# Rotated queries and keys: transposed on VectorE in blocks of 32 by 32, with the blocks moved by DMA through DRAM

## The chip, the cores and the metric

The kernel runs on one core of one Trainium2 chip. The metric is device time in microseconds (us) of one execution; lower is better. All inputs and outputs are float32.

## The reference, cut to what matters

Two blocks of two layers each, at 256 tokens and width 2048. The change touches the first block alone, whose layers hold a differential attention (8 heads, two queries and two keys of 128 each), a stick-breaking attention (16 heads of 128), two branch projections with gates and an output projection. What is computed around the change:

```python
def rms_norm(x, gain):
    xf = x.astype(jnp.float32)
    y = xf * lax.rsqrt(jnp.mean(xf * xf, axis=-1, keepdims=True) + RMS_EPS)
    return (y * gain.astype(jnp.float32)).astype(x.dtype)

def rope(x):
    ...
    x1, x2 = xf[..., : d // 2], xf[..., d // 2:]
    return jnp.concatenate([x1 * cos - x2 * sin, x2 * cos + x1 * sin], axis=-1).astype(x.dtype)

# hybrid_layer
    q = rope(rms_norm(da_q.reshape(b, s, 2 * DA_HEADS, DA_QK_DIM), qk_q_gain))
    k = rope(rms_norm(da_k.reshape(b, s, 2 * DA_HEADS, DA_QK_DIM), qk_k_gain))
    q = (q * (DA_QK_DIM ** -0.5)).reshape(b, s, DA_HEADS, 2, DA_QK_DIM)
    k = k.reshape(b, s, DA_HEADS, 2, DA_QK_DIM)
    ...
    oa = differential_attention(q[:, :, :, 0, :], q[:, :, :, 1, :],
                                k[:, :, :, 0, :], k[:, :, :, 1, :], va, lam)
# differential_attention, a block of 128 queries
        def probs(qb, kt):
            s = jnp.einsum('bhqd,bhkd->bhqk', qb, kt, preferred_element_type=jnp.float32)
            return jax.nn.softmax(jnp.where(causal, s, MASK_VALUE), axis=-1)
        a = probs(qb1, k1t) - lam * probs(qb2, k2t)
        return jnp.einsum('bhqk,bhkd->bhqd', a.astype(vt.dtype), vt)
```

## The kernel before

**Weights.** Every projection streams its weights from DRAM in halves of 512 KB (128 partitions x 1024 columns). `weights` (L71 to L89) loads a half into `raw` (3 buffers) with a DMA that SyncE's queue (SP) issues (L85), ScalarE (ACT) rounds it into `hi` (4 buffers, L86), and VectorE (DVE) writes the remainder into `lo` (4 buffers, L87). A product is made of three matmuls: activations' high part with `hi`, high part with `lo`, low part with `hi`.

**The projections.** `xstat` (L92 to L108) holds the activations still and streams weights: a half gives 12 matmuls of 512 columns (L104 to L106) into an accumulator of two PSUM banks (`acc`, 2 buffers). After each half it calls `tick`. `wstat` (L112) does the same with weights held still; it makes the projections that are wanted with columns on the partitions.

**Ticks.** Attention is written as Python generators that are started with `spawn` and advanced one step by every `tick` (L63), so that their instructions are written between the matmuls of projections. A step is a stretch between two `yield`s. The framework orders all instructions ahead of time from the written order, taken as priority, and from its own model of when each is ready: an engine's list can take an instruction earlier than it is written. Weights have a priority of 400 instructions ahead (L74). Each engine then runs its list in order and waits on semaphores; SP's list holds nearly all DMAs.

**A layer of the first block.** For each of four pairs of heads `layer` (L537) projects q, k, v and z with `xstat` (four times eight halves). After q it starts `da_pair` (L435), which waits for what it needs: it rotates q, then k when `"k"` is there, makes the scores and the probabilities (`da_probs`, L334), evicts v (`evict_v`, L384) and z (`da_gz`), and makes the output (`da_out`). Its result `ua` is read first after four more projections of gates (32 halves).

**A rotation.** `da_rot` (L295) takes the accumulator of one projection (two blocks of 128 tokens, 4 heads of 128 columns). ACT squares it (L304), DVE makes the two products and their sum (L306 to L313) and the sum of squares (L312), GpSimd (POOL) the inverse root (L316 to L318), and for keys DVE scales the rows (L324). Then, for each block of tokens, PE transposes four 128x128 tiles with the identity into a PSUM bank (L329), and ACT copies the bank into `out`, which is `qkT` with columns on the partitions (L330). The scores (L342, L343) read `qkT`.

In a layer there are 8 rotations; the second block has none.

Of the kernel before, what the change touches and what calls it, by code (L numbers as in the profile page):

```python
# [11 lines left out]
F32 = mybir.dt.float32  # L12
# [6 lines left out]
P = 128  # L19
# [15 lines left out]
def bc(ap, shape, axis):  # L35
    return ap.unsqueeze(axis).to_broadcast(shape)
# [133 lines left out]
class Block1(Net):  # L170
# [124 lines left out]
    def da_rot(self, acc, tabs, scaled, res):  # L295
        nc = self.nc
        out = self.w4.tile([P, 4, T], F32, tag="w4", name="qkT")
        c = self.sm.tile([P, 2, 4], F32, tag="s8", name="c")
        ssq = self.sm.tile([P, 2, 4], F32, tag="s8", name="ssq")
        rots = []  # L300
        for tb in range(2):
            pv = acc[:, tb, :]
            sq = self.w2.tile([P, 4, P], F32, tag="w2", name="sq")
            nc.scalar.activation(sq, pv.rearrange("p (s d) -> p s d", s=4), AF.Square, scale=self.r[:, tb : tb + 1])  # L304
            t1 = self.w2.tile([P, 4, P], F32, tag="w2", name="t1")
            nc.vector.tensor_tensor(  # L306
                out=t1, in0=pv.rearrange("p (s d) -> p s d", s=4), in1=bc(tabs[0][:, tb, :], [P, 4, P], 1), op=ALU.mult)
            t2 = self.w2.tile([P, 4, 2, 64], F32, tag="w2", name="t2")
            nc.vector.tensor_tensor(
                out=t2, in0=pv.rearrange("p (s h d) -> p s h d", s=4, h=2)[:, :, ::-1, :],  # L310
                in1=bc(tabs[1][:, tb, :].rearrange("p (h d) -> p h d", h=2), [P, 4, 2, 64], 1), op=ALU.mult)
            nc.vector.tensor_reduce(ssq[:, tb, :], sq, AX.X, ALU.add)  # L312
            nc.vector.tensor_tensor(out=t1, in0=t1, in1=t2.rearrange("p s h d -> p s (h d)"), op=ALU.add)  # L313
            rots.append(t1)
            yield
        self.rsqrt(c, ssq, 128.0 * EPS)  # L316
        for tb in range(2):
            nc.gpsimd.tensor_scalar(c[:, tb, :], c[:, tb, :], self.r[:, tb : tb + 1], None, ALU.mult)  # L318
        yield
        yield  # L320
        if scaled:
            for tb in range(2):
                t1 = rots[tb]
                nc.vector.tensor_tensor(out=t1, in0=t1, in1=bc(c[:, tb, :], [P, 4, P], 2), op=ALU.mult)  # L324
            yield
        for tb in range(2):
            pt = self.ps().rearrange("p (s d) -> p s d", s=4)
            for sh in range(4):
                nc.tensor.transpose(pt[:, sh, :], rots[tb][:, sh, :], self.ident)  # L329
            nc.scalar.copy(out[:, :, tb * P : (tb + 1) * P], pt)  # L330
        yield
        res += [out, c]

    def da_probs(self, qT, kT, cq, aTs):  # L334
# [1029 lines left out]
def build(nc, a, out, opts):  # L1364
    with tile.TileContext(nc) as tc, ExitStack() as ctx:
        dram = ctx.enter_context(tc.tile_pool(name="dram", bufs=1, space=bass.MemoryType.DRAM))
        b = Block1(nc, tc, ctx, a)
# [4 lines left out]
            tp=pool(c1, "tp", bufs=1),  # L1372
            w4=pool(c2, "w4", bufs=6, side="right"), w15=pool(c2, "w15", bufs=8, side="right")))
        x1 = dram.tile([P, 16, T], F32, name="x1")
        xt, xs = [b.tt() for _ in range(4)], []
        b.sqs = b.tp.tile([P, 2, T], F32, tag="sqs", name="sqs")

# [189 lines left out]
```

## Time and profile before

| | |
|---|---|
| median of 3 runs | 3277.18 us (3275.35 to 3278.25) |
| the profiled execution | 3272.04 us |
| its span in the trace | 3270.3 us |
| PE / DVE / ACT busy | 99% / 66% / 51% of the span |
| granted TensorE clock | 0.998 of full speed |
| DMA | 573 MB, mean 175 GB/s |

The profile is of one execution. PE is the matmuls on TensorE, PEld its weight loads, DVE VectorE, ACT ScalarE, POOL GpSimd, SP SyncE with its DMA queue. Matmuls overlap and their ends are modelled, so the start of one matmul after the other tells more than their durations. `out<-in` are the program's names, L and a number a line of the kernel. In a timeline a row has the start (us), the time (us), engine, line, operation and, in brackets, how long the engine was idle just before and what ended that.

### The profile page before, as it was taken

How to read it: one execution, taken by the hardware profiler on the slowest of the kernel's cores; microseconds unless marked ns; L12 is line 12 of the kernel's file. 1: busy time of each engine (PE TensorE's matmuls, PEld its weight loads, DVE VectorE, ACT ScalarE, POOL GpSimd, SP SyncE). 2: the span in 40 equal slices, each digit the busy share in tenths (PEclk: the TensorE clock that was granted, in tenths of full speed). 3: DMA queues.
4: the chain of work that ended last, by engine and by line, in shares of the span. 5: the costliest groups of instructions: out<-in, count | busy, mean ns of one | idle time of the engine just before them, and what ended most of it. 6: DMA issues, size and time to landing. Idle time of an engine off the chain costs nothing.

```text
span 3270.3 us, 48437 instructions
## 1 busy us (share of the span) xinstructions
PE 3243.7 (99%) x19158; PEld 2862.2 (88%) x19158; DVE 2173.0 (66%) x2865; ACT 1656.0 (51%) x2321; POOL 253.2 (8%) x227
## 2 busy tenths in 40 slices
PE   9999999999999999999999999999999999999998
PEld 7888888888888888888888888888889999999998
DVE  7666655566665666566655566665678986689865
ACT  5544444444444454444444444444456675466753
POOL 2010100000000001001100000000013000130003
PEclk9999999999999999999999999999999999999999
DMA  6555556555555666555556655555665534555454
GB/s 227 172 170 171 174 181 193 182 174 175 171 176 182 209 204 194 172 172 170 175 178 192 185 175 173 172 176 182 203 190 181 161 121 143 171 166 160 128 166 141
DMA packets 165189, 573.04 MB, mean 175 GB/s; under 512 B 22497, under 2 KB 25441, under 8 KB 164961
## 3 DMA queue, kind: packets, MB, share of 16 engines
q1 hardware_dynamic: 164816, 569.93, 55.3%
q8 instruction: 150, 2.46, 0.3%
q14 instruction: 79, 0.64, 0.1%
q10 hardware_dynamic: 144, 0.02, 0.0%
HBM read 565.68 MB, written 4.19 MB: 174 GB/s over the span
## 4 chain that ended last, share of the span: by engine, by line
PE 92%; DVE 4%; issue 2%; ACT 1%; DMA 1%; POOL 0%; SPq 0%; POOLq 0%; DVEq 0%; ACTq 0%
PE acc L138 29%; PE acc L140 14%; PE acc L106 8%; PE acc L105 8%; PE acc L104 8%; PE acc L131 6%; PE acc L132 6%; PE acc L133 6%; DVE lo L87 1%; PE acc L137 1%; PE ps L379 1%; DMA raw<-wx 0%; PE ps L329 0%; PE ps L343 0%; PE ps L1166 0%
## 5 line engine op out<-in xcount | busy, mean ns | idle before, releaser
L87 DVE TENSOR_TENSOR lo<-raw,hi 128x1024 fp32r<-128x1024 f32 (+1 forms) x1061 | 1318.0, 1243 | 761.1 <-ACT hi L86 758.6
L86 ACT CAST hi<-raw 128x1024 fp32r<-128x1024 f32 (+1 forms) x1061 | 1114.2, 1050 | 1187.3 <-PE acc L138 444.8
L138 PE MATMUL acc<-T,hi 128*128 128x512 f32 x4096 | 1439.9, 397 | 0.0
L140 PE MATMUL acc<-T,lo 128*128 128x256 f32 x3840 | 1077.7, 281 | 0.0
L138 PEld LDWEIGHTS acc<-T,hi 128*128 128x128 f32 x4096 | 762.0, 188 | 171.6
L140 PEld LDWEIGHTS acc<-T,lo 128*128 128x128 f32 x3840 | 725.7, 189 | 5.8
L104 PE MATMUL acc<-hi,T 128*128 128x512 f32 x1280 | 520.7, 407 | 0.3 <-ACT hi L86 0.3
L131 PE MATMUL acc<-T,hi 128*128 128x272 f32 (+2 forms) x1776 | 519.1, 292 | 0.2 <-DVE w L890 0.2
L132 PE MATMUL acc<-T,hi 128*128 128x272 f32 (+2 forms) x1776 | 508.9, 287 | 0.0
L133 PE MATMUL acc<-T,lo 128*128 128x272 f32 (+2 forms) x1776 | 508.9, 287 | 0.0
L105 PE MATMUL acc<-lo,T 128*128 128x512 f32 x1280 | 505.9, 395 | 2.7 <-DVE lo L87 2.7
L106 PE MATMUL acc<-hi,T 128*128 128x512 f32 x1280 | 505.7, 395 | 0.0
L131 PEld LDWEIGHTS acc<-T,hi 128*128 128x128 f32 x1776 | 335.4, 189 | 2.2 <-DVE w L890 0.4
L132 PEld LDWEIGHTS acc<-T,hi 128*128 128x128 f32 x1776 | 335.4, 189 | 1.6
L133 PEld LDWEIGHTS acc<-T,lo 128*128 128x128 f32 x1776 | 335.5, 189 | 0.1
L105 PEld LDWEIGHTS acc<-lo,T 128*128 128x128 f32 x1280 | 241.6, 189 | 57.6 <-DVE lo L87 4.3
L106 PEld LDWEIGHTS acc<-hi,T 128*128 128x128 f32 x1280 | 240.4, 188 | 56.4
L104 PEld LDWEIGHTS acc<-hi,T 128*128 128x128 f32 x1280 | 241.0, 188 | 54.0 <-ACT hi L86 0.7
L145 ACT COPY sum<-acc 128x512 f32<-128x512 f32 x128 | 75.1, 586 | 221.6 <-PE acc L138 221.6
L146 DVE TENSOR_TENSOR sum<-acc,sum 128x512 f32<-128x512 f32 x128 | 88.5, 692 | 145.0 <-ACT sum L145 145.0
L257 POOL TENSOR_TENSOR sqs<-sqs,sq 128x512 f32<-128x512 f32 x14 | 23.0, 1643 | 856.9 <-ACT sq L256 856.6
L925 ACT ACTIVATE tap<-cpad,pc 128x272 f32<-128x272 f32 x120 | 56.3, 518 | 38.6 <-DVE y L928 37.9
(369 smaller groups left out, 2360.9 us busy)
## 6 DMA issues: line engine op xcount, KB each, us to landing
raw<-ww SPq DMA_DIRECT2D x512, 512.0 KB, 4.4
raw<-wx SPq DMA_DIRECT2D x319, 512.0 KB, 3.9
raw<-w2in SPq DMA_DIRECT2D x160, 512.0 KB, 3.8
raw<-w2out SPq DMA_DIRECT2D x64, 512.0 KB, 4.6
x<-xT SPq DMA_DIRECT2D x4, 512.0 KB, 5.9
x<-x SPq DMA_DIRECT2D x8, 256.0 KB, 3.0
x<-x SPq DMA_DIRECT2D x4, 512.0 KB, 6.2
raw<-pw SPq DMA_DIRECT2D x4, 512.0 KB, 3.7
```

The costliest lines, as they stand in the source:

```text
L86: nc.scalar.copy(hi[:, sl], raw[:, sl])
L87: nc.vector.tensor_tensor(out=lo[:, sl], in0=raw[:, sl], in1=hi[:, sl].bitcast(F32), op=ALU.subtract)
L104: nc.tensor.matmul(o, xh, wh[:, k, :], start=first, stop=False)
L105: nc.tensor.matmul(o, xh, wl[:, k, :], start=False, stop=False)
L106: nc.tensor.matmul(o, xl, wh[:, k, :], start=False, stop=last)
L131: nc.tensor.matmul(o, wh[:, k, cs], xh, start=first, stop=False)
L132: nc.tensor.matmul(o, wh[:, k, cs], xl, start=False, stop=False)
L133: nc.tensor.matmul(o, wl[:, k, cs], xh, start=False, stop=last)
L138: nc.tensor.matmul(both, wh[:, k, cs], x[:, :, kc % 4, lo : lo + n], start=first, stop=last)
L140: nc.tensor.matmul(o, wl[:, k, cs], xh, start=False, stop=False)
L145: nc.scalar.copy(t, acc[:, :, n : 2 * n])
L146: nc.vector.tensor_tensor(out=t, in0=acc[:, :, :n], in1=t, op=ALU.add)
```

## The change

After the rotation, DVE transposes the 128x512 block of each 128 tokens in blocks of 32 by 32 (`nc.vector.transpose`), so that within a block tokens and columns change places and the blocks stay where they are. Two DMAs write the results to a DRAM tile (`rot`, 3 buffers). Two steps later four DMAs read it back, each 32 partitions of `qkT`, with the blocks in the transposed order: runs of 32 values (128 bytes) from DRAM to SBUF. Five more steps pass before the result is handed on. The PE transposes, their PSUM buffers and ACT's copies are gone. The order of the layers, the weights and everything else in the text is as before.

```diff
             yield
+
+        dr = self.dram.tile([2 * P, 4, P], F32, tag="rot", bufs=3, name="rot")
         for tb in range(2):
-            pt = self.ps().rearrange("p (s d) -> p s d", s=4)
-            for sh in range(4):
-                nc.tensor.transpose(pt[:, sh, :], rots[tb][:, sh, :], self.ident)
-            nc.scalar.copy(out[:, :, tb * P : (tb + 1) * P], pt)
-        yield
+            tr = self.w2.tile([P, 4, P], F32, tag="w2", name="tr")
+            nc.vector.transpose(tr.rearrange("p s d -> p (s d)"), rots[tb].rearrange("p s d -> p (s d)"))
+            nc.sync.dma_start(out=dr[tb * P : (tb + 1) * P], in_=tr)
+        yield
+        yield
+        blocks = dr.rearrange("(i a) s (j b) -> j a s i b", a=32, b=32)
+        for j in range(4):
+            r = out[32 * j : 32 * j + 32]
+            nc.sync.dma_start(out=r.rearrange("a s (i b) -> a s i b", b=32), in_=blocks[j])
+        for _ in range(5):
+            yield
         res += [out, c]
...
         x1 = dram.tile([P, 16, T], F32, name="x1")
+        b.dram = dram
```

## Rows read from the trace of the kernel before

**Rows 1.** The page's first part: busy us, share of the span and instructions of each engine.

```profile
PE 3243.7 (99%) x19158; PEld 2862.2 (88%) x19158; DVE 2173.0 (66%) x2865; ACT 1656.0 (51%) x2321; POOL 253.2 (8%) x227
```

**Rows 2.** Busy time by stretch (us, PE, PEld, DVE, ACT, POOL, PEclk, DMA share, GB/s).

```profile
...
100.00:400.00 300.00, 299.94 (x1358) 244.69 (x1357) 188.33 (x253) 146.04 (x221) 32.83 (x42) 1.00 0.55 172
```

**Rows 3.** The waits, 100 to 400 us: us in total, times, longest us.

```profile
...
ACT hi L86 <- PE acc L106: 133.2, 78, 2.4
```

**Rows 4.** One line's instructions, L329: duration ns min/median/max; then what PE waited for.

```profile
...
L329 PE MATMUL ps<-ident,t x128: 270/272/329, 57.0 to 1599.1; 128*128 128x128 f32 x128
...
  DVE t L324: 1.4, 6
```

**Rows 5.** The timeline from 143.5 us: start us, us, what; one rotation of queries.

```profile
...
144.03 0.39 PE L104 MATMUL acc<-hi,T 128*128 128x512 f32 x1
...
144.26 0.39 PE L105 MATMUL acc<-lo,T 128*128 128x512 f32 x1
...
145.18 0.40 PE L106 MATMUL acc<-hi,T 128*128 128x512 f32 x1
...
145.42 1.03 PE L329 MATMUL ps<-ident,t 128*128 128x128 f32 x8
...
146.21 0.48 PE L104 MATMUL acc<-hi,T 128*128 128x512 f32 x1
...
146.52 0.40 PE L105 MATMUL acc<-lo,T 128*128 128x512 f32 x1
...
146.61 1.07 ACT L330 COPY qkT<-ps 128x512 f32<-128x512 f32 x2
```

**Rows 6.** The timeline from 54 us, the first rotation.

```profile
...
58.92 1.05 ACT L86 CAST hi<-raw 128x1024 fp32r<-128x1024 f32 x1 [1.58 <-DMA raw<-wx]
...
59.31 0.63 PE L329 MATMUL ps<-ident,t 128*128 128x128 f32 x4 [1.75 <-DVE t L313]
```

**Rows 7.** The timeline from 150 us, of ACT and then of DVE.

```profile
...
154.86 1.05 ACT L86 CAST hi<-raw 128x1024 fp32r<-128x1024 f32 x1 [1.74 <-PE acc L106]
...
155.94 1.23 DVE L87 TENSOR_TENSOR lo<-raw,hi 128x1024 fp32r<-128x1024 f32 x1 [1.56 <-ACT hi L86]
...
170.47 1.50 DVE L324 TENSOR_TENSOR t<-t,c 128x512 f32<-128x512 f32 x2 [1.96 <-POOL c L318]
```

**Rows 8.** DMA issues of the whole span: xcount, KB each, median us to landing.

```profile
...
raw<-wx SPq DMA_DIRECT2D x319, 512.0 KB, 3.9
...
x<-x SPq DMA_DIRECT2D x8, 256.0 KB, 3.0
...
hx<-metaT SPq DMA_DIRECT2D x1, 128.0 KB, 5.1
...
ng<-ng ACTq DMA_DIRECT2D x1, 16.0 KB, 2.2
```

**Rows 9.** One line's DMA issues each: time of an issue on SP, ns.

```profile
...
L1426 SPq DMA_DIRECT2D x<-x x8: 326/327/330, 1172.6 to 1245.8; - x8
...
L1415 SPq DMA_DIRECT2D hx<-metaT x1: 672/672/672, 2390.2 to 2390.2; - x1
```

**Rows 10.** SP's own waits: 100 to 400 us, then 1150 to 1260 us.

```profile
...
SPq L85 <- DVE lo L87: 245.5, 92, 4.2
...
SPq L1426 <- DVE x L1425: 17.9, 8, 2.4
```

**Rows 11.** Groups of 100 to 400 us (mean ns after the busy us), and line L1058.

```profile
...
L313 DVE TENSOR_TENSOR t<-t,t 128x512 f32<-128x512 f32 x12 | 8.2, 684 | 0.0
...
L1058 DVE STREAM_SHUFFLE t<-t x20: 428/452/497, 2550.5 to 3039.4; 128x272 f32<-128x272 f32 x12, 128x256 f32<-128x256 f32 x8
```

**Rows 12.** One line's instructions each, 130 to 270 us: first and last start.

```profile
...
L342 PE MATMUL ps<-qkT x8: 270/272/275, 175.3 to 183.0; 128*128 128x128 f32 x8
...
L379 PE MATMUL ps<-ident,s x6: 271/272/273, 200.2 to 200.8; 128*128 128x128 f32 x6
...
L387 ACT ACTIVATE v<-acc,r x2: 678/684/689, 183.3 to 183.9; 128x512 f32<-128x512 f32 x2
```

## The prediction

> **What bounds the kernel now.** The first view is the page's busy table: TensorE (PE) is busy for 99% of the span, VectorE (DVE) for 66%, ScalarE (ACT) for 51% [rows 1]. A busy PE proves little by itself, since matmul ends are modelled, so the second view is the table by stretch for the stage in which the rotated queries and keys are made: between 100 and 400 us PE has work in 299.94 of 300 us at full clock, while DVE works 188, ACT 146 and the DMA engines 55% [rows 2]. The third view is the waits of the same stretch: the casts of the weights wait for PE, because PE has to give back one of the four `hi` buffers first [rows 3]. So the supply of weights runs ahead of PE and is held back by it. Whatever takes PE time away in this stage shortens the span; work put on DVE, ACT, the DMA queue (SP) or the DMA engines is free until the weights come late. The question is thus how much PE time goes, and how late the new DMAs make the weights.
>
> **What goes: 128 transposes on PE.** There are 16 rotations (4 pairs, q and k, 2 layers) with 8 transposes each. Their mean duration is 272 ns [rows 4], which would make 34.8 us, but matmuls overlap, so the duration isn't the price. The price is the gap that they make in the stream of weight matmuls. Ordinary matmuls of this stage start 0.23 us apart (144.03, 144.26). Around the 8 transposes of one rotation L106 starts at 145.18 and the second matmul after it, L105, at 146.52: 1.34 us in place of 0.46 [rows 5]. So a rotation costs 0.88 us, or 0.11 us for one transpose, and 16 cost 14.1 us. PE also waits for DVE's scaling of the keys (L324) ahead of six of them, 1.4 us in all [rows 4]; those waits go too. Sum: 15.5 us. The first rotation also stops PE for 1.75 us for DVE [rows 6]. I count that at nothing: in the same microseconds casts wait 1.58 us for a weight load [rows 6], so loads are just in time there and what PE doesn't lose to DVE it can lose to them. It stays as 2 us in the lower end.
>
> The Trainium skill ("VectorE: DVE Perf Modes", section "The three transpose paths") prices a 128x128 transpose on TensorE at 390 ns in bf16. By that figure 128 of them would be an estimate of 50 us and the time about 3227 us; the gap in the row is a quarter of that price, and the row decides.
>
> The 32 evictions by ACT (L330, after the transposes [rows 5]) go as well. ACT is off the path here, so nothing is counted.
>
> **What comes on DVE: 32 block transposes of 128x512.** The trace has no such instruction. Near ones are an addition of the same shape, 0.68 us, and a shuffle within blocks of 32 partitions over 256 or 272 columns, 0.45 us, about one column a cycle [rows 11]. I take 0.69 us, with 0.34 us (two columns a cycle) and 1.4 us (two passes) as ends: 1.4 us a rotation, at most 2.8. DVE has 37% free in the stage [rows 2]. Who stands behind it on DVE is `lo` (L87), which PE needs. Its spare time: a cast starts when a buffer comes free, and `lo` is ready 2.3 us later (cast at 154.86, subtraction from 155.94 for 1.23) [rows 7]. PE still has three tiles of 12 matmuls before it, 3 x 12 x 0.2325 = 8.4 us. So 6.0 us are spare, and even 2.8 us cost nothing.
>
> **What comes on SP and the DMA engines.** Each rotation adds two writes of 256 KB and four reads of 128 KB, each read in 1024 pieces of 128 bytes (32 partitions x 4 heads x 8 blocks). First the issuing: 0.33 us for a write of that size and 0.67 us for the one existing load in many small pieces (`hx<-metaT`, 2048 pieces of 64 bytes) [rows 9], so 2 x 0.33 + 4 x 0.67 = 3.3 us. SP spends 245 of 300 us waiting for DVE to give back a `raw` buffer [rows 10], so it has room.
>
> Then the moving. 1024 pieces over 16 engines are 64 for each engine and read, 256 for the four. The pace of a piece is the number on which this case turns. `hx<-metaT` landed 5.1 us after its issue, and the smallest load (`ng`) took 2.2 us [rows 8]; the 2.9 us between them over 128 pieces an engine are 23 ns. The upper end is the whole 5.1 us, 40 ns. The lower is a plain load of the same bytes: 512 KB of weights land in 3.9 us [rows 8], 1.7 us over the smallest. I take 23 ns, as it is from the only load of this kind, though its source was read in sequence and this one is read in pieces scattered over rows: 256 x 23 ns = 5.9 us of all 16 engines, with 1.7 and 10.2 us as ends.
>
> Who is late then? The weight load queued behind the reads. One tile lasts 2.79 us and the engines are 55% busy [rows 2], so 1.25 us of each tile are idle and the load comes about 5.9 - 1.25 = 4.6 us late, with the writes some 0.3 us more: 4.9 us. What it may be late: a load is issued when the subtraction three tiles before ends, lands 3.9 us later [rows 8], and its cast comes 8.4 - 2.3 - 3.9 = 2.2 us after that; with the 6.0 us behind the cast, 8.2 us. So the reads are covered with 3.3 us to spare, and PE sees nothing of them.
>
> **Added waits.** The reads wait on SP for the writes to land (3.0 us for such a write [rows 8]), and the writes wait for DVE. The existing write of x1 waited 17.9 us for DVE in 8 cases, 2.2 us each [rows 10]. Behind them stand weight loads, which would themselves have waited for a buffer for most of a tile, so little of it counts; 3.3 us are covered.
>
> **What moves.** The generator yields 6 steps more in each rotation. The keys' rotation starts 2 steps later, not 6, because the pair waited for the keys' accumulator anyway; in all the scores come 8 steps (22 us) later. For the pair at 175 us that is about 197 us [rows 12]. The reads: scaling ends at 172.0 [rows 7], the two transposes about 173.4, the writes have landed near 177.5, the reads are issued by 180.5 and moved by 187. So the scores wait for nothing. The last pair has 59 steps before its result is used and needs about 40.
>
> **Sum.** 0 + 0 - 15.5 us. The profiled execution took 3272.0 us (span 3270.3), which gives 3256.5; the median of the runs is 5.1 us above it, so 3277.2 - 15.5 = **3261.7 us**, 0.47% less. A measurement of this kernel tells about 0.2% (6.5 us) from no change.
>
> **Rivals.**
> - *Small pieces are slower than 40 ns (slower).* The mechanism is the same queue: with a pace p the load is late by 256p - 0.95 us, PE stops beyond 8.2 us (p = 36 ns), and the whole gain (0.97 us a rotation) is lost at p = 40 ns. At 50 ns: 11.85 us late, 3.65 us of stop in 16 rotations, 58 us, so 3261.7 + 58 = 3320 us; at 46 ns 3303 us. For it: the source is scattered at steps of 512 bytes and 2 KB, which no load of the trace is. Against it: 64-byte pieces ran at about 23 ns, and the pace would have to double. Chance 0.27. The Trainium skill ("DMA: Bandwidth & Descriptors", section "Specifications") says that below 512 bytes a transfer is done as read-modify-write, which speaks against this change; if every piece cost two accesses the estimate would be this rival's 50 ns. The trace's 64-byte load doesn't show such a doubling, but it went from DRAM to SBUF in sequence only.
> - *SP waits take the place of the transposes (no change).* If the waits for DVE and for the landing put SP 4.3 us behind, the load is 4.9 + 4.3 = 9.2 us late, 1.0 us beyond the cover, 16 us in 16 rotations: 3277 us. For it: the x1 write's waits. Against: SP's own idle time. Chance 0.17.
> - *A later eviction holds the accumulator (slower; the change doesn't do what it says).* With two `acc` buffers the next queries' matmuls need v's, and v's eviction (L387) stands 8 steps later in the code, behind the matmuls that need it. But it ran at 183.3, when v was ready, 17 us before the transposes that stand ahead of it in the code (200.2) [rows 12]; engines other than PE aren't held to the written order. Counted within the slower chance.
>
> **How the numbers follow.** Forecast 0.56 (3256 to 3270), no change 0.17, slower 0.27. Lower end: 2 us of the first rotation and 0.1% of scatter (3 us), 3256. Upper end: through the second rival and, of the first, up to 46 ns, about 3305; some 0.16 lies above and 0.03 below. Chances: faster 0.56, same 0.17, slower 0.27.
>
> **What would show it.** L329 gone, and L104 to L106 0.23 us apart across a rotation; casts that wait for `raw<-wx` for a few us after each group of reads, yet no idle PE; DVE transposes near 0.69 us; reads that land within some 4 to 9 us of issue; PE idle time in 100 to 400 us still under 1 us. It is wrong if PE waits for `lo` or `hi` in that stretch, if reads land 12 us or more after issue, or if PE waits for `qkT` at L342.

## The result: slower by 0.6%

The changed kernel takes 3295.13 us in the median (3290.55 to 3296.62, 4 runs), the kernel before, run beside it, 3276.26 us (3271.21 to 3278.25). The ratio is 1.0059 with an interval of 1.0047 to 1.0071: some 19 us slower, where 15.5 us faster was forecast. About 34 us have to be found.

Lines of the changed kernel that the text names: L309, L312 and L313 products and sums of the rotation, L330 the block transposes on DVE, L331 the writes, L337 the reads, L350 the scores, L374 the last product of the probabilities, L387 their transposes on PE, L424 the root's last step on POOL (`so`), L429 the gated output `u` on DVE, L438 its transposes on PE.

The page's first part, of after, against [rows 1]: PE is busy for as much of the span, so this row doesn't show the loss.

```profile
PE 3247.2 (99%) x19030; PEld 2854.1 (87%) x19030; DVE 2193.5 (67%) x2897; ACT 1640.9 (50%) x2289; POOL 246.4 (7%) x227
```

The table by stretch, of after (us; busy time of PE, PEld, DVE, ACT and POOL; granted clock, DMA share, GB/s), against [rows 2]:

```profile
100.00:400.00 300.00, 294.50 (x1294) 236.51 (x1293) 195.22 (x264) 140.03 (x206) 28.77 (x42) 0.99 0.67 193
...
300.00:500.00 200.00, 192.93 (x948) 159.49 (x947) 121.23 (x163) 93.45 (x141) 10.96 (x20) 0.98 0.61 178
...
1500.00:1700.00 200.00, 191.99 (x886) 156.41 (x885) 123.34 (x167) 90.87 (x138) 16.01 (x24) 0.97 0.63 183
```

PE, which lost 0.06 us in 300 before, now loses 5.5 us there, and 7 to 8 us in each of the two stretches in which a layer's last pair ends. The granted clock falls too. The waits of PE over the whole span, of after (us in total, times, longest):

```profile
PE ps L438 <- DVE u L429: 8.5, 7, 3.3
PE ps L387 <- DVE s L374: 5.5, 4, 1.6
PE acc L104 <- DVE t L309: 4.9, 3, 3.6
...
PE acc L105 <- DVE lo L87: 3.0, 4, 1.0
PE acc L138 <- ACT v L395: 2.3, 1, 2.3
...
PE ps L350 <- DMA raw<-ww: 0.7, 1, 0.7
```

and of before:

```profile
PE acc L105 <- DVE lo L87: 2.7, 3, 1.0
PE ps L329 <- DVE t L313: 1.7, 1, 1.7
```

So the weights are not late for PE: it waits 3.0 us for `lo`, as before. The new waits are for the products of the attention itself: `u`, `s`, `t` and `v`, 21.2 us; the kernel before has one such wait, the 1.7 us at L329. At the scores, where PE would wait for the new reads, it waits 0.7 us once, which the profile puts down to a weight load.

The second part of the loss is the clock. The table by stretch, of after, at four places just behind such waits and at two in the second block (columns as above):

```profile
157.25:160.66 3.41, 3.41 (x12) 2.62 (x11) 1.96 (x5) 0.85 (x2) 0.00 (x0) 0.50 0.41 154
...
443.96:450.79 6.83, 6.43 (x17) 4.68 (x18) 2.03 (x6) 2.29 (x7) 0.41 (x2) 0.50 0.27 85
1597.67:1601.08 3.41, 2.86 (x10) 2.09 (x9) 3.41 (x7) 1.18 (x2) 2.83 (x4) 0.50 0.28 102
1683.00:1689.83 6.83, 5.73 (x15) 4.13 (x16) 2.26 (x7) 2.17 (x7) 0.00 (x0) 0.50 0.33 109
2648.97:2652.38 3.41, 3.41 (x18) 3.41 (x17) 3.38 (x9) 2.74 (x9) 0.00 (x0) 0.50 0.38 124
3044.92:3048.33 3.41, 3.41 (x14) 3.18 (x15) 3.34 (x8) 3.00 (x13) 0.00 (x0) 0.50 0.41 131
```

The granted clock is 0.50 there (the lower of the two levels, 1.2 GHz). In the first four stretches PE works 18.4 us at it and so loses 9.2 us. With the 21.2 us of waits this is 30 us of the 34. The last two, 3.4 us of loss, lie in the second block, whose code did not change; the trace of before has no such stretch there, those of e2_nodma and e18_mid2 have one each (2611.8 and 2614.2 us). They are not counted as the change's. The load `hx<-metaT`, issued as the second block begins, tells the blocks apart, of after and then of e2_nodma (the experiment without the DMAs, below):

```profile
L1424 SPq DMA_DIRECT2D hx<-metaT x1: 643/643/643, 2411.1 to 2411.1; - x1
```

```profile
L1417 SPq DMA_DIRECT2D hx<-metaT x1: 671/671/671, 2375.1 to 2375.1; - x1
```

Before, it is issued at 2390.2 us [rows 9]. So 20.9 us of the 24.5 by which the two traces differ (3294.8 and 3270.3 us of span) arise in the first block.

The operations themselves, of after: the DVE transposes, and the issues of the DMAs (KB each, median us to landing), against [rows 4, 8, 11]:

```profile
L330 DVE STREAM_TRANSPOSE tr<-t x32: 664/700/705, 62.3 to 1615.7; 128x512 f32<-128x512 f32 x32
```

```profile
rot<-tr SPq DMA_DIRECT2D x32, 256.0 KB, 4.7
qkT<-rot SPq DMA_DIRECT2D x64, 128.0 KB, 5.3
```

The transposes and the reads cost what was forecast; a write landed after 4.7 us where 3.0 had been taken. What was not forecast is where the DMAs stand. The timeline of SP's queue from 157 us, of after, second pair (start us, us; x the loads in a row):

```profile
157.00 0.92 SPq L331 DMA_DIRECT2D rot<-tr  x2
159.79 0.56 SPq L337 DMA_DIRECT2D qkT<-rot  x1
162.72 3.85 SPq L85 DMA_DIRECT2D raw<-wx  x2
166.63 0.56 SPq L337 DMA_DIRECT2D qkT<-rot  x1
169.00 7.85 SPq L85 DMA_DIRECT2D raw<-wx  x3
...
184.10 0.56 SPq L337 DMA_DIRECT2D qkT<-rot  x1
...
191.92 0.90 SPq L331 DMA_DIRECT2D rot<-tr  x2
...
216.81 0.56 SPq L337 DMA_DIRECT2D qkT<-rot  x1
```

Between one read and the next stand two or three weight loads, and each waits until a buffer comes back. One rotation's four reads thus last from 159.8 to 184.1, the keys' blocks, transposed by 177.7, are written at 191.9, and the last read is issued at 216.8. The scores come at 224.3 us, not at 197 (before: 175.3 [rows 12]). L350 from 140 to 240 us, of after:

```profile
L350 PE MATMUL ps<-qkT x8: 272/274/275, 224.3 to 226.4; 128*128 128x128 f32 x8
```

And this is what the lateness leads to: the timeline, of after, at the end of the first pair (start us, us; in brackets the idle time before and what ended it):

```profile
148.85 0.74 DVE L374 SCALAR_TENSOR_TENSOR s<-s,nrl 128x128 f32<-128x128 f32 x2
...
150.87 1.15 POOL L195 TENSOR_SCALAR c<-ssq 128x8 f32<-128x8 f32 x1 [75.23 <-DVE ssq L312]
...
153.85 0.58 POOL L318 TENSOR_SCALAR c<-c,r 128x4 f32<-128x4 f32 x2
...
155.63 0.20 POOL L424 TENSOR_TENSOR so<-so,rh 128x2 f32<-128x2 f32 x1
155.87 0.48 DVE L429 SCALAR_TENSOR_TENSOR u<-ps,so,gz 128x256 f32<-128x256 f32 x1 [3.95 <-POOL so L424]
...
156.27 1.29 DVE L330 STREAM_TRANSPOSE tr<-t 128x512 f32<-128x512 f32 x2
...
156.50 0.41 PE L438 MATMUL ps<-ident,u 128*128 128x128 f32 x2 [3.35 <-DVE u L429]
```

Two things are to be seen. First, the late end of pair 1 and the rotation of pair 2 run in one another: on POOL the rotation's roots (150.87 to 154.4) stand right ahead of the pair's `so`, which starts at 154.5 though ACT had its sums at 152.0, and behind it DVE idles 3.95 us and PE 3.35 us; and on DVE the queries' block transposes (L330), whose data have been there since L313 at 140.0, stand behind the pair's `s` and `u`. Second, PE's transposes follow their producer with nothing between: `u` starts at 155.87, L438 at 156.50. In the timeline of before, the same two (L421, L430) are 9.7 us apart:

```profile
115.32 0.48 DVE L421 SCALAR_TENSOR_TENSOR u<-ps,so,gz 128x256 f32<-128x256 f32 x1 [0.89 <-POOL so L416]
...
125.02 0.60 PE L430 MATMUL ps<-ident,u 128*128 128x128 f32 x4
```

At the last pair of a layer no rotation follows, and PE waits there too. The timeline of PE, of after, last pair of the first layer:

```profile
442.80 0.30 PE L387 MATMUL ps<-ident,s 128*128 128x128 f32 x1 [1.62 <-DVE s L374]
```

A wait of 1.14 us for the next `s` follows at 444.24, then the stretch of 6.83 us at the half clock. The second layer has the same pair of waits (1682.5 and 1684.0) and such a stretch. Before, the last pair's `s` of the first layer is made from 391.0 us and PE's transposes of it start at 396.0, with no wait.

### The profile page after: what moved, and what is told of

It reads as the page before. It is cut to its first block, busy times and chain, and to the rows that moved or that the text cites. A ratio compares the mean times of both kernels' runs of the same rounds, so it can differ in the third digit from the quotient of the medians.

```text
span 3294.8 us, 48315 instructions
## 1 busy us (share of the span) xinstructions
PE 3247.2 (99%) x19030; PEld 2854.1 (87%) x19030; DVE 2193.5 (67%) x2897; ACT 1640.9 (50%) x2289; POOL 246.4 (7%) x227
## 4 chain that ended last, share of the span: by engine, by line
PE 86%; DVE 7%; ACT 2%; issue 2%; DMA 1%; POOL 1%; SPq 0%; POOLq 0%; DVEq 0%; ACTq 0%
PE acc L138 29%; PE acc L140 14%; PE acc L106 8%; PE acc L105 8%; PE acc L104 8%; PE acc L131 5%; PE acc L132 5%; PE acc L133 5%; DVE lo L87 2%; PE acc L137 1%; DVE y L922 1%; ACT hi L86 1%; PE ps L387 1%; DVE y L936 1%; PE ps L351 0%
```

## The experiments

The letters in the texts on record are names of theories; each text says what its letters stand for. Each ratio is to the kernel before, run on the same chip.

**The price of the PE transposes (e2_nodma).** The change without its DMAs: DVE transposes straight into `qkT`, with all written steps kept. It leaves out the movement of the blocks between partitions.

```diff
-            tr = self.w2.tile([P, 4, P], F32, tag="w2", name="tr")
-            nc.vector.transpose(tr..., rots[tb]...)
-            nc.sync.dma_start(out=dr[tb * P : (tb + 1) * P], in_=tr)
+            nc.vector.transpose(out[:, 2 * tb : 2 * tb + 2, :]..., rots[tb]...)
...
-            nc.sync.dma_start(out=r..., in_=blocks[j])
```

> The changed kernel without its DMAs: VectorE's block transpose writes straight into qkT, all steps kept. It leaves out the movement of the blocks between partitions. It prices the removed transposes of TensorE with nothing late behind them. If the sum of the prediction is right: 3262 us (15.5 us less than before). If the gap between matmuls overstates what they are worth: 3270 us. If the DVE work or the added steps alone are the loss: 3290 us or more.

Measured: 3259.77 us, ratio 0.9956 (0.9940 to 0.9973), 12.8 us less than the 3272.53 beside it. The table by stretch, of e2_nodma:

```profile
100.00:300.00 200.00, 200.00 (x893) 163.10 (x892) 134.20 (x189) 94.41 (x139) 19.15 (x28) 1.00 0.55 175
300.00:500.00 200.00, 199.88 (x1021) 168.74 (x1020) 124.75 (x160) 99.89 (x149) 11.76 (x20) 1.00 0.57 180
```

The gain of the sum is there: 12.8 us in the medians, and 15.1 us in the first block by the load of `metaT` above (2375.1 against 2390.2 us). DVE's 32 transposes cost PE nothing, and with the same written steps PE has no gaps. All of the loss comes with the DMAs.

**Steps alone and traffic alone (e3_steps, e4_traffic).** Both are the kernel before; one with six more steps in each rotation, the other with the six DMAs of each rotation into a tile that nobody reads.

```diff
-        yield
+        for _ in range(7):
+            yield
```

```diff
+        dr = self.dram.tile([2 * P, 4, P], F32, tag="rot", bufs=3, name="rot")
+        spare = self.w4.tile([P, 4, T], F32, tag="w4", name="spare")
+        for tb in range(2):
+            nc.sync.dma_start(out=dr[tb * P : (tb + 1) * P], in_=rots[tb])
...
+            nc.sync.dma_start(out=r.rearrange("a s (i b) -> a s i b", b=32), in_=blocks[j])
```

> The kernel before with six more steps (yields) at the end of each rotation and nothing else. Theory L: steps that only move the written place cost nothing, 3277 us within 0.2%. Rival S (the pair's end falls into the next pair's rotation, whatever moved it there): 3285 us or more, with PE waiting for the rotation's or the output's DVE work.

> The kernel before with the traffic of the change added as dead work: the rotated rows are written to DRAM and read back in the same 128-byte runs into a spare tile that nobody reads; TensorE's transposes stay. Theory L: nobody waits for it, 3277 us within 0.4%. Theory T: the weights come late and the time is 3292 to 3310 us.

Measured: 3274.61 us, 1.0003 (0.9994 to 1.0012), and 3275.91 us, 1.0006 (0.9997 to 1.0015). In e3_steps the scores of the second pair come at 195.1 us, 20 us later than before, and that costs nothing. The table by stretch, of e4_traffic:

```profile
100.00:300.00 200.00, 199.97 (x907) 163.21 (x906) 126.45 (x171) 96.88 (x146) 21.65 (x28) 1.00 0.68 196
```

The DMA engines are as busy as in after (0.67) and PE loses nothing. The small pieces by themselves are harmless to the time; the loss needs something that waits for them.

**The DMAs ahead of the weight loads (e1_prio, e7_reads, e10_qfirst).** If the place in SP's list makes the pair late, putting the DMAs ahead of the loads should help: writes and reads of all rotations, reads alone, or those of the queries alone.

```diff
-            nc.sync.dma_start(out=r.rearrange("a s (i b) -> a s i b", b=32), in_=blocks[j])
+            with self.tc.high_priority(offset=1200):
+                nc.sync.dma_start(out=r.rearrange("a s (i b) -> a s i b", b=32), in_=blocks[j])
```

> The changed kernel with one edit: the two writes and four reads of each rotation stand in SP's list ahead of the weight loads (priority 1200 ahead), so that the four reads follow one another. Theory L (the list puts each of them behind two or three weight loads, the scores come some 50 us late in place of 22, and the rest of the pair loses the steps that kept PE from waiting): the scores of the second pair start near 197 us, PE's idle time in the two stages of the pairs falls from some 20 us to under 3, time 3262 to 3268 us. Theory T (the traffic of small pieces delays the weights, wherever it stands): about 3295 us or more, with PE waiting for lo or hi.

> The changed kernel with only the four reads of a rotation ahead of the weight loads in SP's list; the writes keep their place. Theory H (in e1_prio the write stood at the head of SP's list and waited up to 12 us for DVE with loads behind it, which made the weights late): SP's wait for the transpose falls from 96 us to under 40, the casts' wait for raw falls from 233 us by half, and the time is between the two, 3275 to 3300 us. Rival (the four reads in a row are themselves what delays the loads): the casts' wait for raw stays near 233 us and the time near 3312 us.

> The changed kernel with the DMAs of the queries' rotations alone ahead of the weight loads in SP's list; the keys' keep their place. Theory L (lateness is made by the DMAs queued one behind the other): the keys' write no longer queues behind the queries' reads, the scores of the second pair start near 205 to 212 us in place of 224, the idle time of TensorE in the pairs falls below 10 us, and the time is 3272 to 3284 us. Theory H (what stands ahead of the loads makes the weights late): casts wait longer for raw and the time is 3295 us or more.

Measured: 3312.16 us, 1.0115 (1.0100 to 1.0130); 3304.05 us, 1.0090 (1.0075 to 1.0106); 3294.88 us, 1.0065 (1.0050 to 1.0080). The scores of the second pair did come earlier, at 189.5, 183.1 and 203.1 us, but the time did not fall. The waits from 100 to 400 us, of e1_prio, first of PE, then of SP:

```profile
PE acc L105 <- DVE lo L87: 9.7, 5, 3.2
...
SPq L332 <- DVE tr L330: 38.4, 12, 12.2
```

Now it is the other fault: a write stands in SP's queue before DVE has made its data, up to 12.2 us, the weight loads stand behind it, and PE waits 3.2 us at a time for `lo` (0.06 us in 300 before). SP's queue of e1_prio shows it: two loads at 161.89, nothing until the write at 175.19.

```profile
161.89 1.09 SPq L85 DMA_DIRECT2D raw<-wx  x2
175.19 0.92 SPq L332 DMA_DIRECT2D rot<-tr  x2
```

With the queries alone it is the same at smaller size (SP's wait 32.9 us in the stretch, longest 10.1; PE 8.3 us for `lo`). With the reads alone the writes were left in place, and yet SP waits for DVE almost as long (33.1 us in the stretch, longest 10.1; 82.6 against 96.2 over the whole span, where under 40 was expected), and the time is just above the range that was expected for it; so e7_reads does not separate writes from reads. So on one queue neither place is free: behind the loads the DMAs are late, ahead of them the loads are. Earlier scores alone were not the cure.

**Only the queries by DRAM (e9_queries, e13_qprio).** Keys stay with PE; e13_qprio has the queries' DMAs ahead of the loads, as above.

```diff
+        if scaled:
+            for tb in range(2):
+                pt = self.ps().rearrange("p (s d) -> p s d", s=4)
...
+        else:
+            dr = self.dram.tile([2 * P, 4, P], F32, tag="rot", bufs=3, name="rot")
```

> Only the queries go through DRAM; the keys are transposed by TensorE as before. Theory L (the keys' write and reads queue behind the queries' reads in SP's list, and so the pair is late): the scores come 10 to 20 us later than before in place of 50, TensorE's idle time in the pairs stays under 4 us, and half the gain is left: 3265 to 3272 us. Rival (each rotation through DRAM costs by itself): half the loss, 3283 to 3288 us.

> Only the queries through DRAM, with their DMAs ahead of the weight loads in SP's list; the keys by TensorE. In e9_queries the scores waited for the last read of the queries. Theory L: the reads end some 10 us before the keys are ready, no wait of the scores, idle time of TensorE in the pairs under 2 us, and half of what the transposes cost is gained: 3264 to 3268 us against 3273 before. Theory H: SP's waits make the weights late and the time is 3275 us or more.

Measured: 3276.06 us, 1.0009 (1.0000 to 1.0019), and 3279.95 us, 1.0017 (1.0007 to 1.0026). Half the transposes gone should give 6 us; e9_queries, with 3 us more than the kernel beside it, lies between the two ranges that were expected. PE waits for the reads themselves there, over the whole span:

```profile
PE ps L358 <- DMA qkT<-rot: 5.2, 5, 2.0
```

These waits are the larger part of the some 9 us between the gain that was expected and the time that came. In e13_qprio these waits are gone; the time fits the theory that the weights are late, but PE waits only 5.5 us for `lo` over the whole span (2.7 before), so the rest of its loss stays open.

**Is it the buffers? (e12_w2_11)** The pool from which `t`, `tr` and `u` come, with 11 buffers in place of 7.

```diff
-w2=pool(c1, "w2", bufs=7)
+w2=pool(c1, "w2", bufs=11)
```

> The changed kernel with 11 buffers in the pool w2 in place of 7 (the rotations' products, the transposed rows and the output's u share it). Theory W (the late output holds w2 and so the next rotation starts late and gives its accumulator back late): the waits of L104 and L138 for t and v (6.9 us) go, and the queries' rotation starts where its projection ends; time 3275 to 3288 us. Rival (w2 isn't short; the lists are only packed): 3292 to 3298 us with the same waits.

Measured: 3292.14 us, 1.0058 (1.0041 to 1.0074), the queries' transposes of the second pair still at 154.5 us and PE's waits for `u`, `s`, `t` and `v` at 20.4 us. Not the buffers.

**PE's transposes of `s` and `u` later (e5_later).** They get a priority 500 instructions behind, so that PE would come to them when the data are there.

```diff
-            aTs.append(self.transpose3(ss[2 * hh]))
+            with self.tc.high_priority(offset=-500):
+                aTs.append(self.transpose3(ss[2 * hh]))
```

> The changed kernel, DMAs as they are, with TensorE's transposes in the pair's later part (of the probabilities and of the output) given a priority 500 instructions later, so that they stand further down in TensorE's list. Theory S (the lost slack: in the changed kernel these stand in the list right behind the DVE work that they read, and TensorE waits for it): the waits of these transposes for u and s (some 12 us in the changed kernel) and the half-clock stretches behind them go, time 3265 to 3280 us. Rival A (the accumulators that are given back late, waits of L104 and L138 for t and v, are the cause): these waits stay or grow and the time stays near 3295 us.

Measured: 3340.65 us, 1.0203 (1.0188 to 1.0218), a miss for both sides. The waits of PE over the whole span, of e5_later:

```profile
PE acc L104 <- DVE t L309: 20.0, 7, 4.4
```

The pair's end came later still, the next rotation behind it too (queries' transposes at 178.2 us, against 156.3), and PE now waits for the rotation to give its accumulator back (`t`, L309); it still waits 14.2 us for `u`. That a later end went with a later next rotation turned the question to the order of the two.

**The number of steps (e8_steps1, e15_steps6, e11_steps7).** One, six or seven steps behind the reads in place of five.

```diff
-        for _ in range(5):
+        for _ in range(7):
             yield
```

> The changed kernel with one step in place of five behind the reads: 8 steps fewer in a pair. Theory L (the reads' place in SP's list decides when the scores run, not the written step): scores of the second pair still near 224 us and the time within 0.3% of the changed kernel, 3285 to 3305 us. Rival (the written steps make the pair late): scores some 11 to 22 us earlier and 3265 to 3280 us.

> The changed kernel with seven steps in place of five behind the reads. Theory S (the pair's later steps are overdue when the scores at last run, so nothing spaces them): more written steps bring the written place nearer to the real one, the scores stay near 224 us, the waits for u and s shrink, 3275 to 3290 us. Rival (one step made it 24 us slower only through a chance order): within 3290 to 3320 us.

> The changed kernel with six steps after the reads in place of five, so two more in a pair. It shows where the time turns between five (3295 us) and seven (3262 us). Theory R: the turn is a step and not a slope, since either the late end of the pair stands ahead of the next rotation or it doesn't: within 5 us of one of the two, with queries' transposes of the second pair near 156 or near 142 us accordingly. Rival D: half of the gain, 3274 to 3284 us.

| steps | us | ratio | queries' transposes, pair 2 | scores, pair 2 |
|---|---|---|---|---|
| 1 | 3319.50 | 1.0137 (1.0120 to 1.0154) | 161.6 | 227.7 |
| 5 (after) | 3295.13 | 1.0059 (1.0047 to 1.0071) | 156.3 | 224.3 |
| 6 | 3263.64 | 0.9965 (0.9952 to 0.9978) | 139.1 | 204.5 |
| 7 | 3261.58 | 0.9961 (0.9946 to 0.9976) | 142.5 | 207.2 |

With one step PE waits twice for `s`, for 8.5 and 8.7 us, both times at the last pair of a layer (445.1 and 1694.4 us). Its waits over the whole span, of e8_steps1:

```profile
PE ps L386 <- DVE s L373: 17.1, 2, 8.7
```

From five steps to six some 30 us go, from six to seven 2 us. That is a switch, not a slope, and the queries' transposes switch with it. e11_steps7 came out below both ranges that were expected (3275 us and more), and its scores moved to 207.2 us where 224 was expected; e8_steps1 came out above its range (3285 to 3305 us), though its scores stayed as expected. Fewer steps did not bring the scores forward: their place is set by SP's list, not by the step in which they are written.

**Four steps where they cannot help the reads (e16_mid, and e18_mid2, the same kernel once more for its trace).** Five steps behind the reads as in after; four more between the last score and the first work on the probabilities.

```diff
             ss.append(s)
             yield
+        for _ in range(4):
+            yield
         nc.vector.tensor_tensor(out=nmx, in0=nmx, in1=cq, op=ALU.mult)
```

> The changed kernel with four more written steps in each pair, put between the last score and the first work on the probabilities; the rotation with its five steps, the DMAs and all else are unchanged. Theory R (order of the late end of a pair against the next rotation): what costs time is that the pair's last products on VectorE, GpSimd and ScalarE are written ahead of the next pair's rotation, so that they go first once the pair is late. Four more steps put them behind it wherever they stand: next queries' transposes back from 156.3 to about 143 us, the scores of the second pair at 205 to 215 us in place of 224, TensorE busy over 199.5 of 200 us in 100 to 300 us, time 3260 to 3272 us. Rival D (the added steps help because the reads get more steps before the scores are written): nothing is gained here, 3290 to 3300 us, scores of the second pair still near 224 us.

> The same kernel as e16_mid, for a trace that can be compared line by line: theory R expects queries' transposes of the second pair at 139 to 147 us, its scores at 205 to 215 us and TensorE busy over 199.5 of 200 us in 100 to 300 us; rival D expects 156, 224 and under 197.

Measured: 3260.35 us, 0.9956 (0.9940 to 0.9973); and 3260.67 us in the single run beside 3276.08. The table by stretch, of e18_mid2:

```profile
100.00:300.00 200.00, 200.00 (x888) 162.36 (x887) 133.52 (x181) 97.24 (x144) 21.73 (x28) 1.00 0.69 205
```

PE loses nothing any more, with the same DMAs. The timeline at the end of the first pair, of e18_mid2 (L376 is after's L374, L431 its L429):

```profile
140.61 0.61 POOL L195 TENSOR_SCALAR c<-ssq 128x8 f32<-128x8 f32 x1 [66.44 <-DVE ssq L312]
...
142.32 1.30 DVE L330 STREAM_TRANSPOSE tr<-t 128x512 f32<-128x512 f32 x2
...
145.64 0.74 DVE L376 SCALAR_TENSOR_TENSOR s<-s,nrl 128x128 f32<-128x128 f32 x2
...
152.69 0.88 DVE L431 SCALAR_TENSOR_TENSOR u<-ps,so,gz 128x256 f32<-128x256 f32 x2 [1.82 <-POOL so L426]
```

The rotation of pair 2 goes first on POOL and DVE (L330 at 142.32, not 156.27), then the end of pair 1; `u` is made at 152.7, earlier than in after, because POOL is free, and PE's transposes of it start at 159.7, 7.0 us after it. The scores of pair 2 come at 206.3 us though no read got more steps; L350 from 140 to 240 us, of e18_mid2:

```profile
L350 PE MATMUL ps<-qkT x8: 270/272/275, 206.3 to 208.4; 128*128 128x128 f32 x8
```

The theory that the steps work by giving room to the reads falls. SP's list is not the same as in after, though: the queries' reads leave within 15.6 us (148.1 to 163.7, one or two loads between them) in place of 24.3. And at the last pair, which has no rotation behind it, the waits are gone as well; its scores start at 404.3 us in place of 427.6.

**The order without steps (e17_rotfirst).** The rotation's work on ACT, DVE and POOL gets a priority of 200 instructions ahead; the steps stay five.

```diff
-            nc.vector.transpose(tr..., rots[tb]...)
+            with self.tc.high_priority(offset=200):
+                nc.vector.transpose(tr..., rots[tb]...)
...
+        with self.tc.high_priority(offset=200):
+            self.rsqrt(c, ssq, 128.0 * EPS)
```

> The changed kernel with its five steps, but the rotation's work on ScalarE, VectorE and GpSimd (squares, products, inverse roots, scaling of keys, block transposes) has a priority of 200 instructions ahead; the DMAs and the written steps are unchanged. Theory R: the next rotation then goes ahead of the late end of the pair before it, as with seven steps, and the time falls to 3260 to 3275 us; queries' transposes of the second pair at 139 to 145 us in place of 156. If it is R but the DMAs' place decides too, 3275 to 3288 us with the transposes early. Rival D (only the distance of the reads or the number of steps counts): transposes early and the time still 3290 to 3300 us.

Measured: 3278.13 us, 1.0011 (1.0002 to 1.0020), about half of what was lost. The expected place was a miss: the timeline of DVE, of e17_rotfirst,

```profile
157.21 0.48 DVE L433 SCALAR_TENSOR_TENSOR u<-ps,so,gz 128x256 f32<-128x256 f32 x1 [3.86 <-POOL so L428]
157.61 1.29 DVE L334 STREAM_TRANSPOSE tr<-t 128x512 f32<-128x512 f32 x2
```

still has the transposes behind `u`. The sums of squares moved ahead of the `s` products (147.4, before 149.5 in after), the transposes did not, and why they did not is not shown. DVE idles as long ahead of `u` (3.86 us) though POOL is done with the roots at 153.1 and itself waits for ACT; so the roots are not needed for that idle time. PE's wait of 3.35 us became one of 0.95 us, and the scores of the second pair stayed at 224.6. The waits of 1.62 and 1.14 us at the last pair stand in the first layer and are gone in the second. So this run moved only a part of the order and gained only a part of the time.

## Why the prediction was wrong

**The step that failed** is "What moves": "the reads are issued by 180.5 and moved by 187. So the scores wait for nothing. The last pair has 59 steps before its result is used and needs about 40." It took SP to issue a read when its data are there. SP runs a list in order, and the list has two or three weight loads between any two reads, each of which waits for a buffer; that waiting was even in view [rows 10], and was read as room for the DMAs, where it was time that the DMAs would have to stand in line. The last read left at 216.8 us instead of 180.5, the scores came 27 us after the forecast.

**What the lateness cost** was not in the sum at all. 20 us of it are free, as e3_steps shows. In after the second pair's scores come 49 us later than before, and the end of the pair then runs into other work. At the first three pairs of a layer this is the next pair's rotation, on the same DVE and POOL, and with five steps the end goes first on DVE. At the last pair no rotation follows, and yet it loses most: PE waits 2.3 us for `v` (first layer) and 1.62 and 1.14 us for `s` in each layer, 7.8 of the 21.2 us, and 12.2 us of its work behind them run at the half clock, 6.1 of the 9.2 us. So some 14 of the 30 us arise where no rotation follows.

What is shown is that the DMAs make the loss (e2_nodma), that traffic, buffers and steps in the kernel before do not (e4_traffic, e12_w2_11, e3_steps), and that it hangs on when the late pair's work runs: four steps behind the scores, which leave the written places of the DMAs as they are, return some 33 us, all of these waits with them, and six or seven steps behind the reads do about the same. That the order of the end and the next rotation is the cause is shown only in part. The four steps do several things at once: they put the rotation first, bring the last pair's scores forward by 23 us, and put PE's transposes of `u` 7.0 us behind it. No run separates these; e17_rotfirst, which was to show the order without steps, moved a part of it and returned about half of the time. That the lists are made so because the pair's end is written ahead of the next rotation and overdue is argued from the framework's use of the written order. How the loss divides between POOL's roots, DVE's order and PE's transposes directly behind their producers stays open. So do about 4 of the 34 us, which neither the waits nor the clock hold (some 6 of 36.0 us if the first blocks of after and e2_nodma are compared by their loads of `metaT`).

Point by point:

- *PE transposes, -15.5 us.* Right: 15.1 us in the first block of e2_nodma's trace and 12.8 us in its medians, where the gap in the timeline and the waits gave 15.5; with the DMAs, 11 to 14 us are left in e15_steps6, e11_steps7 and e16_mid. Per transpose this is 0.10 us (12.8 / 128) to 0.12 us (15.1 / 128). The Trainium skill ("VectorE: DVE Perf Modes", section "The three transpose paths") has 390 ns for one in bf16. The trace of these float32 transposes, which stand in a stream of other matmuls, does not agree.
- *The first rotation, counted at nothing.* The wait of 1.75 us [rows 6] became one of 1.0 us for `t` (L309) in its place.
- *DVE, 0.69 us each, free.* Right: 0.700 us in the median, and e2_nodma's PE is without gaps.
- *DMA engines, 5.9 us a rotation, covered.* Right: the share rose from 0.55 to 0.67 of 300 us with six rotations, 36 us or about 6.0 us each, writes included; reads landed after 5.3 us; e4_traffic cost nothing. The casts now wait 38.0 us for loads and 96.3 for PE, where it was 133.2 for PE [rows 3], and PE sees nothing of it: that sign came as named. The Trainium skill ("DMA: Bandwidth & Descriptors", section "Specifications") has pieces under 512 bytes done as read-modify-write; with 128-byte pieces no run here shows a cost of it in the kernel's time.
- *First rival, small pieces over 40 ns (0.27, slower).* The sign came out, by another mechanism, and so by luck.
- *Second rival, SP's waits (0.17, no change).* It looked at the right queue and the wrong victim: SP waits 16.7 us for the writes and 8.8 us for DVE in 100 to 400 us. In after the weights are not late (3.0 us for `lo`); only in e1_prio, e7_reads and e10_qfirst do the waits for DVE make them so.
- *Third rival, the late eviction of `v`.* It does occur: PE waits 2.3 us for L395, once. The same mechanism, an accumulator given back late, is behind the 4.9 us of waits for the rotation's `t` (L309); together they are a third of the 21.2 us. It was given no time of its own.
- *The cover of "59 steps ... about 40".* It counted when the last pair's result is used, not whether PE's transposes in the pair would stand right behind the work that they read. PE has no wait for the result; its waits came inside the pair.
- *The range*, 3256 to 3305, reaches the time only by the room left for rivals that did not happen; that 3295 lies in it is luck.

**A version that beats both.** With four steps more behind the scores (e16_mid) or six or seven steps behind the reads (e15_steps6, e11_steps7) the kernel takes 3260 to 3264 us, 0.9956 to 0.9965 of the kernel before. Their intervals overlap. More than seven steps, and the DMAs on another engine's queue, were not tried.

## What to carry to other kernels

When a step on the compute path is replaced by DMAs, price their place in the queue's list before their bytes: a queue that idles because its next entry waits for a buffer has no room for what stands behind that entry. And when a producer comes later, look at what its consumers then run into on every engine that they share with the next round, and at what stands right behind them: here the added work was free by itself, and when the late work ran cost some 33 us, which a few written steps gave back. A gain that is there in the variant without the DMAs and gone with them says that the place of the DMAs, not the exchange of engines, is what has to be worked on.

## What the runs showed of the hardware

- Behind idle times of PE of 1.6 and 1.1 us (442.80, 444.24) or 3.35 us (156.50) the granted clock was 0.50 for 6.83 or 3.41 us; matmuls of 512 columns then started 0.43 us apart in place of 0.23 (157.59 to 158.45). The wait of 3.35 us thus cost 1.7 us more (3.41 us of work at half the rate), the two of 2.8 us together 3.2 us more (6.43 us of work).
- A block transpose of 128x512 float32 on DVE takes 0.70 us, like an addition of that shape (0.68 us).
- A read of 128 KB in 1024 pieces of 128 bytes landed 5.3 us after its issue (2.8 to 7.1) beside the stream of weights. In e4_traffic the DMA engines' share from 100 to 300 us was 0.68 in place of 0.55, and PE lost 0.03 us there.
